# Input projection of a diffusion block: two chunks in one written order, weights loaded by GpSimd, first norm reordered

## The chip, the core and the metric

The kernel runs on one core of a Trainium2 chip. The metric is the device time of one execution in microseconds; a kernel's time is the median of several runs. The core has five engines that run beside each other, each with its own stream of instructions: TensorE (matmul; PE in the profile, PEld for its weight loads), VectorE (DVE), ScalarE (ACT), GpSimd (POOL) and SyncE (SP), which here only issues DMAs. They meet through semaphores. Matmuls write PSUM, eight banks of 128 x 512 numbers; everything else lies in SBUF, which has 128 partitions.

## The reference

One layer of a diffusion backbone over 512 latent tokens of width 2048 with 256 context tokens. What the change touches is its head:

```python
mod_l = (jax.nn.silu(c) @ w_ada[l] + b_ada[l])[:, None, :]
sh_a, sc_a, gt_a, sh_f, sc_f, gt_f = jnp.split(mod_l, 6, axis=-1)
h_l = modulate(rms_norm(x, g_mix_norm[l]), sh_a, sc_a)      # h * (1 + scale) + shift
qa_l, kva_l, kr_l, cb_l, cc_l, ch_l = split_projection(h_l @ w_in[l])
```

Here x is 512 x 2048 and w_in 2048 x 3904 (31 blocks of 128 columns, the last padded). After it come a low-rank attention with the context, a gated short convolution, an output projection, and a gated MLP (5504 wide) with a convolution, all in float32.

## The kernel before, in words

Activations lie transposed: 16 tiles `xs[j]` of 128 channels by 512 tokens. Each float32 factor is split into a high and a low part (`h`, `l`; fp32r), and a product takes three matmuls: high by high, high by low, low by high (`mm3`, L187 to L189). ScalarE makes the high part of a weight group (`split`, L166: up to four blocks of 128 x 128, 512 columns), VectorE the low part (L167).

**Modulation.** `mod` has 96 columns of 128 numbers. Column t is a dot product of a 128 x 2048 slab of w_ada (1 MB, loaded as two halves, the `ada` tiles, four of which fit in SBUF) with `sv`, Silu of c laid over all partitions. VectorE does it as two operations of 128 x 1024 with an accumulator (L241) and a tiny addition (`total`, L235). Tile j of h needs columns 16 + j (scale) and j (shift): `prep(j)` issues the four dots, scales x by the norm's factor `rl` on VectorE (L435), applies scale and shift on ScalarE (L438), and splits the result (L337, L338).

**Start.** SP loads io (identity and ones), c, sixteen x tiles, c_ctx, the small vectors `sm`, then ada halves and weights, in one queue. TensorE spreads c and c_ctx over the partitions by matmuls with a row of ones (L413), ScalarE takes Silu of them (L414). For the norm ScalarE squares each x tile and VectorE adds it to a sum (L354, L355); TensorE adds that over the partitions (`rs`, L316), ScalarE takes the root, VectorE the reciprocal, TensorE transposes it back (L299), and a copy of that is `rl`.

**Projection.** Its depth of 16 tiles is cut in three chunks, of 2, 4 and 10 (`KCH`), so that it can begin when two tiles of h are there. In each chunk the first six column blocks (`G`) are done row by row, tile after tile of h, into six PSUM banks; the other 25 one after another. Chunk one's results are copied to `acc` by ScalarE (L539), later ones added to it by VectorE (L541). Weights come by SP in loads of up to 1 MB into two buffers `raw`. The `prep`s of later tiles stand in a table after certain blocks (`todo`). A scheduler sets each engine's order; the instructions marked with `keep` hold the order in which they were written among themselves, and so do the loads that SP issues in the first two chunks. In chunk three VectorE also does the 64 dots of the context's modulation (`ctx_mods`, L530).

**Later places.** `late_dot` does the remaining 56 columns of `mod` beside attention and the output projection; `sv` is stored to HBM (`sv_d`) for the MLP stage, which reads it back; `ufr` are the first weights of the MLP.

Of the kernel before, what the change touches and what calls it, by code (L numbers as in the profile page):

```python
# [10 lines left out]
F32 = mybir.dt.float32  # L11
F32R = mybir.dt.float32r
AF = mybir.ActivationFunctionType
ALU = mybir.AluOpType
# [17 lines left out]
G = 6  # L32

# [39 lines left out]
def block_kernel(ctx, tc, xt, ctxt, ctxn, c, c_ctx, w_ada, small, w_in, w_inc, w_q, w_kv, w_out,  # L73
# [55 lines left out]
    def first_banks(nm):  # L129
        turn[:] = 5, None  # L130
        r = [sml(f"{nm}{g}") for g in range(4)]
        b = big(f"{nm}4")
        return r + [b[:, :512], b[:, 512:]]
# [15 lines left out]
    def load(src, n, name):  # L149
# [5 lines left out]
        fetch_to(raw[:, :n], src)  # L155
# [77 lines left out]
    def total(col, t, dst):  # L233

        V.scalar_tensor_tensor(out=dst, in0=col[:, 0:1], scalar=col[:, 1:2], in1=s("b_ada", t), op0=ALU.add, op1=ALU.add)  # L235

    def dot_v(raw, vec, t, dst, nm):

        col = tiny(2, f"dv{nm}{t}")
        for i, r in enumerate(raw):  # L240
            V.scalar_tensor_tensor(out=r, in0=r, scalar=1.0, in1=vec[:, i * 1024:(i + 1) * 1024], op0=ALU.mult, op1=ALU.mult, accum_out=col[:, i:i + 1])  # L241
# [158 lines left out]
    with ExitStack() as pa:  # L400
# [4 lines left out]
        def silu_rows(src, dst, nm):  # L405

            row = wp.tile([P, 2048], F32, tag="raw", bufs=2, name=nm)[0:1, :]
            fetch_to(row, src)
            for g in range(4):
                if g % 2 == 0:  # L410
                    both = big(f"{nm}{g}")
                ps = both[:, (g % 2) * 512:(g % 2 + 1) * 512]
                PE.matmul(ps, ones[0:1, :], row[:, g * 512:(g + 1) * 512], start=True, stop=True)  # L413
                A.activation(dst[:, g * 512:(g + 1) * 512], ps, AF.Silu)  # L414
# [7 lines left out]
        hl = {}  # L422

        def mods(j):
            ada(16 + j)
            ada(j)

        def prep(j):
            mods(j)
            modulate(j)  # L430

        def modulate(j):

            xr = xs[j]
            keep(V.tensor_tensor(out=xr, in0=xr, in1=rl, op=ALU.mult))  # L435
            sc = tiny(1, f"sc{j}")
            scale_of(sc, s("g_mix", j), mod[:, 16 + j:17 + j])
            A.activation(xr, xr, AF.Identity, bias=mod[:, j:j + 1], scale=sc)  # L438
            hl[j] = hilo(xr, T, f"h{j}")


        SP.dma_start(io, consts[:, KCW:])
        silu_rows(c, sv, "c")
        xs = []
        ssq = None
        for j in range(NK):
            xs.append(t2([P, T], F32, f"xr{j}"))
            fetch_to(xs[j], xt[:, j * T:(j + 1) * T])
            ssq = add_squares(ssq, xs[j], T, f"xs{j}")
        silu_rows(c_ctx, svc, "cc")  # L450
        fetch_to(sm, small)
        rms([ssq], D, T, rl)
# [1218 lines left out]
```

## Time and profile before

| what | value |
|---|---|
| runs, median (lowest to highest) | 2132.49 us (2132.07 to 2137.19) |
| the profiled execution, its time | 2139.37 us |
| its span | 2137.6 us |
| granted TensorE clock, mean | 0.993 |
| TensorE busy | 2091.0 us, 98% |
| VectorE busy | 1826.5 us, 85% |
| ScalarE, GpSimd busy | 1047.5 us, 117.2 us |
| first projection matmul | at 29.63 us |
| first matmul of chunk three | at 171.23 us |

In rows of the timeline the first number is the start in us, the second the duration, then engine, line, operation, output<-inputs and shapes; in brackets the idle time of the engine just before, and what ended it. In rows by stretches each engine has its busy time and in brackets its instructions, then come the granted clock as a share, the DMA engines' busy share and GB/s. Matmuls overlap: a row's duration is longer than the distance to the next start, and the distance is the cost.

### The profile page before, as it was taken

Reading aid. Unit: us, or ns where it says so; the run is one execution under the profiler, and the core shown is the slowest. Engines: PE = TensorE matmul, PEld = TensorE weight load, DVE = VectorE, ACT = ScalarE, POOL = GpSimd, SP = SyncE. Lnnn points to the kernel's source line nnn. Section 1 sums busy time; section 2 is a strip of 40 time slices with the busy share of each in tenths; the row PEclk is TensorE's granted clock in tenths of the full one; section 3 lists DMA queues with packets and bytes.
Section 4 is the critical chain, followed back from the end, with each engine's and each line's share of the span. In section 5 each row is a group of like instructions: output and inputs, shape, how many; then the busy total and the mean of one; then the engine's idle time right before and its main releaser. Section 6 shows DMA issues by size and latency. Waiting matters only on the chain.

```text
span 2137.6 us, 35318 instructions
## 1 busy us (share of the span) xinstructions
PE 2091.0 (98%) x13268; PEld 1881.8 (88%) x13268; DVE 1826.5 (85%) x3024; ACT 1047.5 (49%) x1715; POOL 117.2 (5%) x144
## 2 busy tenths in 40 slices
PE   7999999999999999999999999999999999999997
PEld 4688788888988888999999999999999889999997
DVE  7998987778896989898999999999999658888887
ACT  5533333555552337565555555555655433333445
POOL 0000000000000100011000000000000000000000
PEclk9999999999999999999999999999999999999999
DMA  8989886334459986577788888788888989878684
GB/s 331 343 279 329 276 275 195 126 128 152 166 188 353 348 283 220 142 217 207 230 238 232 233 233 244 224 234 234 235 229 229 362 306 307 250 231 239 197 236 134
DMA packets 170177, 513.75 MB, mean 240 GB/s; under 512 B 18963, under 2 KB 23315, under 8 KB 164371
## 3 DMA queue, kind: packets, MB, share of 16 engines
q1 hardware_dynamic: 133364, 418.14, 57.7%
q0 software_dynamic: 17408, 59.25, 14.1%
q10 hardware_dynamic: 19232, 34.09, 4.2%
q8 instruction: 104, 1.70, 0.3%
q14 instruction: 69, 0.56, 0.1%
HBM read 464.22 MB, written 46.14 MB: 239 GB/s over the span
## 4 chain that ended last, share of the span: by engine, by line
PE 90%; DVE 4%; DMA 3%; ACT 2%; issue 1%; SPq 0%; DVEq 0%; ACTq 0%; POOLq 0%
PE pp L187 4%; PE pp L189 4%; PE pp L188 4%; PE d L187 1%; PE o L187 1%; PE d L188 1%; PE o L188 1%; PE d L189 1%; PE o L189 1%; PE uf L187 1%; PE uf L189 1%; PE uf L188 1%; PE of L187 1%; PE of L188 1%; PE of L189 1%; PE pf L188 1%
## 5 line engine op out<-in xcount | busy, mean ns | idle before, releaser
L1151 POOL DMA_DIRECT2D u_s<-in_w_up x80 | 68.6, 857 | 684.0 <-DMA u_s<-in_w_up 378.1
L263 DVE SCALAR_TENSOR_TENSOR ada<-ada,sv 128x1024 f32<-128x1024 f32 x68 | 82.1, 1220 | 11.4 <-DMA ada<-in_w_ada 11.2
L166 ACT CAST w_0h<-rw 128x512 fp32r<-128x512 f32 (+1 forms) x63 | 38.3, 618 | 108.3 <-PE pp L188 67.6
L241 DVE SCALAR_TENSOR_TENSOR ada<-ada,sv 128x1024 f32<-128x1024 f32 x64 | 77.6, 1220 | 2.2 <-DMA ada<-in_w_ada 2.1
L530 DVE SCALAR_TENSOR_TENSOR ada<-ada,svc 128x1024 f32<-128x1024 f32 x64 | 76.0, 1219 | 2.5 <-DMA ada<-in_w_ada 2.4
L167 DVE TENSOR_TENSOR w_0l<-rw,w_0h 128x512 fp32r<-128x512 f32 (+1 forms) x63 | 42.7, 683 | 22.8 <-ACT w_0h L166 22.6
L263 DVE SCALAR_TENSOR_TENSOR ra<-ra,sv 128x1024 f32<-128x1024 f32 x44 | 52.5, 1219 | 1.1 <-DMA ra<-in_w_ada 1.1
L1265 DVE TENSOR_TENSOR u<-u,u_s 128x1024 f32<-128x1024 f32 x40 | 48.8, 1220 | 0.7 <-DMA u_s<-in_w_up 0.5
L1266 DVE TENSOR_TENSOR u<-u,u 128x1024 f32<-128x1024 f32 x40 | 48.7, 1218 | 0.0
L793 POOL TENSOR_TENSOR gr<-gr,half 128x8 f32<-128x8 f32 x4 | 10.1, 2524 | 630.1 <-DVE gr L792 538.2
L764 ACT CAST pth<-t 128x384 fp32r<-128x384 f32 x64 | 28.6, 485 | 26.4 <-PE t L761 26.4
L1075 DVE TENSOR_TENSOR tp<-a,tp 128x256 fp32r<-128x256 f32 x90 | 37.7, 419 | 3.3 <-ACT tp L1074 3.3
L1074 ACT CAST tp<-a 128x256 fp32r<-128x256 f32 x90 | 35.7, 403 | 5.5 <-DMA yl6h<-y_d 4.2
L1038 ACT ACTIVATE g<-g 128x512 f32<-128x512 f32 x43 | 27.3, 634 | 18.3 <-DVE g L1032 18.0
L541 DVE TENSOR_TENSOR acc<-acc,pp 128x512 f32<-128x512 f32 x50 | 34.1, 683 | 2.1 <-PE pp L189 2.1
L765 DVE TENSOR_TENSOR ptl<-t,pth 128x384 fp32r<-128x384 f32 x64 | 33.2, 550 | 2.6 <-ACT pth L764 2.6
L745 DVE TENSOR_REDUCE mn<-s 128x1 f32<-128x768 f32 x32 | 30.4, 953 | 4.9 <-PE s L734 4.6
L1030 ACT ACTIVATE g<-cg,sm 128x512 f32<-128x512 f32 x40 | 32.6, 815 | 0.0
L1030 ACT ACTIVATE a<-ca,sm 128x512 f32<-128x512 f32 x40 | 32.1, 802 | 0.0
L748 ACT ACTIVATE p<-s,mn 128x768 f32<-128x768 f32 x32 | 29.3, 916 | 1.6 <-DVE mn L745 1.3
L1031 DVE SCALAR_TENSOR_TENSOR g<-cg,sm,g 128x511 f32<-128x511 f32 x40 | 29.8, 746 | 0.0
L1032 DVE SCALAR_TENSOR_TENSOR g<-cg,sm,g 128x511 f32<-128x511 f32 x40 | 29.8, 746 | 0.0
(10238 smaller groups left out, 8925.0 us busy)
## 6 DMA issues: line engine op xcount, KB each, us to landing
ada<-in_w_ada SPq DMA_DIRECT2D x196, 512.0 KB, 5.7
u<-in_w_up SPq DMA_DIRECT2D x120, 512.0 KB, 8.9
w<-t_d SPq DMA_DIRECT2D x161, 256.0 KB, 5.3
u_s<-in_w_up SPq DMA_DIRECT2D x80, 512.0 KB, 4.0
u_s<-in_w_up POOLq DMA_DIRECT2D x80, 512.0 KB, 9.6
t_d<-tp ACTq DMA_DIRECT2D x126, 256.0 KB, 5.9
v<-in_w_dnw SPq DMA_DIRECT2D x72, 384.0 KB, 5.1
ra<-in_w_ada SPq DMA_DIRECT2D x22, 1024.0 KB, 4.8
```

The costliest lines, as they stand in the source:

```text
L166: A.copy(out=hi[:, :n], in_=raw[:, a:a + n])
L167: V.tensor_tensor(out=lo[:, :n], in0=raw[:, a:a + n], in1=hi[:, :n].bitcast(F32), op=ALU.subtract)
L187: PE.matmul(ps, w[0], x[0], start=first, stop=False, skip_group_check=on_top)
L188: PE.matmul(ps, w[0], x[1], start=False, stop=False, skip_group_check=on_top)
L189: PE.matmul(ps, w[1], x[0], start=False, stop=last, skip_group_check=on_top)
L241: V.scalar_tensor_tensor(out=r, in0=r, scalar=1.0, in1=vec[:, i * 1024:(i + 1) * 1024], op0=ALU.mult, op1=ALU.mult, accum_out=col[:, i:i + 1])
L263: keep(V.scalar_tensor_tensor(out=r, in0=r, scalar=1.0, in1=svs[i], op0=ALU.mult, op1=ALU.mult, accum_out=lc[:, t % 4:t % 4 + 1] if i else ...
L530: keep(V.scalar_tensor_tensor(out=raw[q], in0=raw[q], scalar=1.0, in1=svc[:, q * 1024:(q + 1) * 1024], op0=ALU.mult, op1=ALU.mult, accum_o ...
L1030: A.activation(u, src, AF.Identity, bias=s("fb", m), scale=s("fw", 86 + m))
L1151: G_.dma_start(r[-1], src[more], accum_op=ALU.add)
L1265: V.tensor_tensor(out=a11, in0=a11, in1=s1, op=ALU.add)
L1266: V.tensor_tensor(out=a12, in0=a12, in1=a11, op=ALU.add)
```

## The change

The first two chunks are written out as one stream of groups of up to four blocks, with every instruction of VectorE, ScalarE and TensorE kept in that order. Chunk one's row-by-row part has eight column blocks instead of six (`GCH`; the host's layout of w_in follows). A group's weights are split two groups ahead of its matmuls. `raw` loads go through GpSimd's DMA queue, in all three chunks, except the very first, which SP brings in two halves; the first GpSimd load stands behind a tiny copy on GpSimd that waits for `mod`'s column 17. Five steps of `preps` (four dots, a low part) are dealt out among the groups; tiles 14 and 15 come in chunk three.

At the start, io and c are loaded by ScalarE's queue; c_ctx is no longer spread by TensorE but loaded over all partitions by one DMA in chunk two. The Silu's table is loaded at once. The squares are summed in two parts; the transposed factor is used for x tile 0 straight from PSUM; ScalarE writes the high parts of tiles 0 and 1 directly. 27 matmuls on a copy of x (`warm`) into a bank that nobody reads (`idle`) stand among the norm's. The store of `sv` is kept in its written place, after the last `late_dot`.

TensorE's start, before; `c` and `cc` are the two rows being spread, `rs` the norm's sums (L316) and transposes (L299):

```order
L413 MATMUL c_108<-c,io 128x512
L413 MATMUL cc_194<-cc,io 128x512
L413 MATMUL cc_199<-cc,io 128x512
L413 MATMUL cc_194<-cc,io 128x512
L413 MATMUL cc_199<-cc,io 128x512
L316 MATMUL rs<-io,xs0t 128x1 x4
L299 MATMUL rs<-io,rr 128x128 x4
L187 MATMUL pf_222<-h0h,wf_0h 128x512
```

And now:

```order
L421 MATMUL c_106<-c,io 128x512
L510 MATMUL idle<-warm,ones_r 128x512 x14
L514 MATMUL rs<-io,xs_161 128x1 x4
L510 MATMUL idle<-warm,ones_r 128x512 x7
L514 MATMUL rs<-io,xs_229 128x1 x4
L510 MATMUL idle<-warm,ones_r 128x512
L541 MATMUL rs<-io,rr 128x128 x4
L510 MATMUL idle<-warm,ones_r 128x512 x5
L727 MATMUL pf_296<-h0h,w0h 128x512
```

The `cc` matmuls are gone from ahead of the norm's, and the idle ones have come in.

VectorE between the last square and tile 1's low part, now (`ada` rows are dots, L682 low parts of weights, L474 of h):

```order
L523 TENSOR_TENSOR xs_229<-xs_229,xs_233 128x512
L539 RECIPROCAL rr<-rr 128x4
L454 SCALAR_TENSOR_TENSOR ada_149,dv_216<-ada_149,sv 128x1024
L243 SCALAR_TENSOR_TENSOR mod<-dv_216,sm 128x1
L454 SCALAR_TENSOR_TENSOR ada_151,dv_259<-ada_151,sv 128x1024
L545 TENSOR_TENSOR xr_114<-xr_114,rs 128x512
L454 SCALAR_TENSOR_TENSOR ada_153,dv_259<-ada_153,sv 128x1024
L243 SCALAR_TENSOR_TENSOR mod<-dv_259,sm 128x1
L682 TENSOR_TENSOR w0l<-rf_155,w0h 128x512
L461 SCALAR_TENSOR_TENSOR sc_280<-mod,sm 128x1
L474 TENSOR_TENSOR h0l<-xr_114,h0h 128x512
L682 TENSOR_TENSOR w1l<-rf_155,w1h 128x512
```

Three of tile 0's four dots now stand behind the reciprocal; before, all four stood ahead of it.

The weight loads of the first chunks, which stood on SP among the ada loads, are GpSimd's first work after its constants:

```order
L705 COPY late<-mod 128x1
L159 DMA rw_368<-in_w_in 128x2048
L159 DMA rw_469<-in_w_in 128x2048
L159 DMA rw_585<-in_w_in 128x1792
L159 DMA rw_709<-in_w_in 128x1536
L159 DMA rw_779<-in_w_in 128x1536
```

Nothing but these loads and that copy is in GpSimd's stream until attention.

The diff, cut to its core:

```diff
+GCH = [8, 6, 6]
...
-        def silu_rows(src, dst, nm):
+        def broadcast_row(src, nm):
 
             row = wp.tile([P, 2048], F32, tag="raw", bufs=2, name=nm)[0:1, :]
-            fetch_to(row, src)
+            A.dma_start(row, src)
+            r = [sml(f"{nm}{g}") for g in range(4)]
...
+        def scaled(j, by):
+
+            x, sc = xs[j], tiny(1, f"sc{j}")
+            keep(V.scalar_tensor_tensor(out=sc, in0=mod[:, 16 + j:17 + j], scalar=1.0, in1=s("g_mix", j), op0=ALU.add, op1=ALU.mult))
+            if by is not None:
+                keep(V.tensor_tensor(out=x, in0=x, in1=by, op=ALU.mult))
+            hl[j] = tuple(t2([P, T], F32R, f"h{j}{z}") for z in "hl")
+            if j < 2:
+                keep(A.activation(hl[j][0], x, AF.Identity, bias=mod[:, j:j + 1], scale=sc))
+            keep(A.activation(x, x, AF.Identity, bias=mod[:, j:j + 1], scale=sc))
+            if j >= 2:
+                keep(A.copy(out=hl[j][0], in_=x))
...
+        def preps(js):
+            for j in js:
+                for t in (16 + j, j):
+                    for i in range(2):
+                        dot(t, i)
+                        if (t, i) == (j, 1):
+                            scaled(j, rl)
+                        yield
+                low(j)
+                yield
+
+        A.dma_start(io, consts[:, KCW:])
+        cps = broadcast_row(c, "c")
+        keep(A.activation(tiny(1, "silu"), eps, AF.Silu))
...
+        while len(xs) < 12:
+            x_load_in()
+        ada_half()
+        while len(xs) < NK:
+            x_load_in()
+        fetch_to(sm[:, :112], small[:, :112])
+        for _ in range(3):
+            ada_half()
+        raw0 = load(w_in[:, :2 * GCH[0] * P], 2 * GCH[0] * P, "rf00", halves=True)
...
+            if j == 13:
+                dot(16, 0)
+                warm_up(4)
+                sums(parts[0], True, False)
+                warm_up(3)
+            elif 8 <= j:
+                warm_up(2)
+        keep(A.activation(tiny(1, "root"), eps, AF.Sqrt))
+        sums(parts[1], False, True)
...
+        def split_group(i):
+            ci, bs, off, size, b = stream[i]
+            if off not in raws:
+                raws[off] = load(w_in[:, off:off + size * P], size * P, f"rw{off}", G_)
+            n = len(bs) * P
+            pool, bufs = (p_sb, 1) if i % 5 == 4 else (wp, 4)
+            hi, lo = (pool.tile([P, 512], F32R, tag="w" + z, bufs=bufs, name=f"w{i}{z}") for z in "hl")
+            src = raws[off][:, b * P:b * P + n]
+            keep(A.copy(out=hi[:, :n], in_=src))
+            keep(V.tensor_tensor(out=lo[:, :n], in0=src, in1=hi[:, :n].bitcast(F32), op=ALU.subtract))
+            ready[i] = hi, lo
...
+        for i, (ci, bs, off, size, b) in enumerate(stream):
+            if i < 2:
+                for _ in range(2):
+                    next(one)
+                if i == 1:
+                    keep(G_.tensor_copy(out=tiny(1, "late"), in_=mod[:, 17:18]))
+            else:
+                for n in range(len(ready), min({2: 4}.get(i, i + 3), len(stream))):
+                    split_group(n)
+                    if n == 2:
+                        next(one)
...
+            for key in out_of:
+                evac_now(*key, banks.pop(key))
+            if ci == 0 and i >= 2:
+                for _ in range(1 + (i % 3 != 0)):
+                    if not {2, 3, 4, 5} <= done:
+                        next(todo)
+            elif ci == 1 and 13 not in done:
+                next(todo)
+                if b + 4 >= size or size == 12:
+                    if 13 not in done:
+                        next(todo)
+            if ci == 1 and i == 24:
+                fetch_to(svc, c_ctx[0].partition_broadcast(P))
...
-    SP.dma_start(sv_d, sv)
+    keep(SP.dma_start(sv_d, sv))
```

260 lines of the change are left out of this document (171 added, 89 removed).

## The prediction

> **What bounds the kernel now.** I read the page's busy shares first, then the busy time by stretches of the first 180 us.
>
> ```profile
> span 2137.6 us, 35318 instructions
> PE 2091.0 (98%) x13268; PEld 1881.8 (88%) x13268; DVE 1826.5 (85%) x3024; ACT 1047.5 (49%) x1715; POOL 117.2 (5%) x144
> 30.00:40.00 10.00, 9.23 (x27) 6.17 (x26) 8.54 (x18) 2.89 (x5) 0.00 (x0) 1.00 0.82 326
> 40.00:50.00 10.00, 10.00 (x43) 8.15 (x44) 8.58 (x18) 4.95 (x9) 0.00 (x0) 1.00 0.81 257
> 50.00:60.00 10.00, 6.86 (x22) 4.67 (x21) 8.56 (x15) 5.34 (x10) 0.00 (x0) 0.76 1.01 403
> 60.00:70.00 10.00, 9.32 (x37) 7.20 (x35) 7.36 (x16) 4.93 (x9) 0.00 (x0) 0.90 0.73 258
> 100.00:120.00 20.00, 20.00 (x88) 16.21 (x87) 20.00 (x38) 6.56 (x12) 0.00 (x0) 1.00 0.83 281
> 180.00:200.00 20.00, 20.00 (x87) 16.21 (x87) 14.04 (x25) 10.82 (x19) 0.00 (x0) 1.00 0.89 309
> ```
>
> The columns are PE, PEld, DVE, ACT, POOL (busy us, instructions), clock, DMA share, GB/s. TensorE is the bound of the whole, with 46.6 us (2137.6 - 2091.0) not busy. From 100 us it is full, 88 matmuls in 20 us; in 30 to 70 us it does 129 in 40 us. That front part is what the change rewrites. The timeline there:
>
> ```profile
> 15.67 7.16 PE L413 MATMUL cc<-cc,io 1*128 1x512 f32 x8 [3.72 <-DMA cc<-in_c_ctx]
> 19.02 0.69 DVE L355 TENSOR_TENSOR xs0t<-xs0t,xs 128x512 f32<-128x512 f32 x1
> 22.76 1.86 PE L316 MATMUL rs<-io,xs0t 128*128 128x1 f32 x8
> 28.11 0.81 ACT L438 ACTIVATE xr<-xr,mod,sc 128x512 f32<-128x512 f32 x1 [1.04 <-DVE xr L435]
> 28.96 0.62 ACT L337 CAST h0h<-xr 128x512 fp32r<-128x512 f32 x1
> 29.63 2.07 PE L187 MATMUL pf<-h0h,wf_0h 128*128 128x512 f32 x4 [3.21 <-ACT h0h L337]
> 44.05 0.39 PE L189 MATMUL pp<-h0h,w_0l 128*128 128x512 f32 x1
> 51.26 0.40 PE L188 MATMUL pp<-h1l,w_0h 128*128 128x512 f32 x1
> 52.88 0.62 ACT L166 CAST w_0h<-rw 128x512 fp32r<-128x512 f32 x1 [5.96 <-DMA rw<-in_w_in]
> 57.30 0.80 PE L187 MATMUL pp<-h0h,w_0h 128*128 128x512 f32 x1 [1.23 <-ACT acc L539]
> 58.32 0.63 PE L189 MATMUL pp<-h0h,w_0l 128*128 128x512 f32 x1
> 61.31 0.63 PE L187 MATMUL pp<-h1h,w_0h 128*128 128x512 f32 x1
> 171.23 0.39 PE L187 MATMUL pf<-h6h,wf_0h 128*128 128x512 f32 x1
> ```
>
> The squares were summed at 19.71 us (19.02 + 0.69), but the matmuls that sum them over the partitions (`rs`) start at 22.76: they stand behind those that spread c_ctx (`cc`). The first projection matmul is at 29.63. Between 44.05 and 51.26 lie 31 starts, 0.2326 us each; between 58.32 and 61.31 lie 7, 0.427 each, where the granted clock fell to 0.76 after the waits at 52 to 57 us, which end with weights that came late (ScalarE waited 5.96 us).
>
> Chunks one and two have 31 x 6 x 3 = 558 matmuls, 129.8 us at 0.2326. The matmul at 171.23 has 546 projection matmuls ahead of it in program order, so that 558 are done at 171.23 + 12 x 0.2326 = 174.0. So 174.0 - 29.63 - 129.8 = **14.6 us** are lost between the first matmul and there, and what comes later waits little. At most these 14.6 and some of the 29.6 ahead of them can be won.
>
> **The start.** Removed ahead of the norm: the c_ctx row's eight passes (7.16 us of TensorE) and four Silus; SP's loads of io and c go to ScalarE's queue, so x starts one issue earlier (it began at 1.58, after io at 0.75); but half an ada tile goes ahead of the last four x tiles, 0.52 MB or 1.3 us at the 402 GB/s of
>
> ```profile
> 10.00:20.00 10.00, 6.28 (x8) 2.11 (x7) 8.83 (x15) 8.17 (x16) 0.00 (x0) 1.00 1.04 402
> 0.75 0.40 SPq L442 DMA_DIRECT2D io<-in_consts  x1
> 1.58 9.56 SPq L145 DMA_DIRECT2D xr<-in_xt  x16
> 6.23 1.28 ACT L414 ACT_TABLE_LOAD   x1
> 6.25 0.69 DVE L355 TENSOR_TENSOR xs0t<-xs0t,xs 128x512 f32<-128x512 f32 x1 [5.33 <-ACT xs L354]
> 8.68 10.25 DVE L355 TENSOR_TENSOR xs0t<-xs0t,xs 128x512 f32<-128x512 f32 x13 [1.73 <-ACT xs L354]
> 99.95 1.22 DVE L241 SCALAR_TENSOR_TENSOR ada<-ada,sv 128x1024 f32<-128x1024 f32 x1
> 101.09 0.08 DVE L241 DVE_READ_ACCUMULATOR ada<-ada,sv 128x1 f32 x1
> 101.09 0.69 DVE L167 TENSOR_TENSOR w_0l<-rw,w_0h 128x512 fp32r<-128x512 f32 x1
> 101.70 1.28 DVE L541 TENSOR_TENSOR acc<-acc,pf 128x512 f32<-128x512 f32 x2
> ```
>
> The adds take 0.79 us each (10.25 / 13), a dot 1.14 before the next starts, a 128x512 VectorE operation 0.60. The first add was at 6.25 and then waited 1.73 for ScalarE, which loaded the Silu's table at 6.23; now the table is loaded first. Thirteen adds from about 5.5 end near 15.9, the first dot near 17.1, the last add (last x near 17) near 18.2. Sums 0.9 to 1.9, square root and reciprocal 0.6, so 20 to 20.5. Then VectorE has, ahead of the first matmul, two dots, the scaling of x, one dot, `w0l`, two tiny totals: 3 x 1.15 + 2 x 0.60 + 0.4 = 5.1, and ScalarE's one pass that writes h0h itself 0.8. First matmul at **26.3**, 3.3 earlier. Bounds: 25.6 (x is in on time), 29.3 (the seven idle matmuls ahead of the second sum run at 0.427 instead of 0.2326, 1.4 us, and the sums at the slow end).
>
> **The second x tile.** 24 matmuls on h0 last 5.6, to 31.9. h1 needs, on VectorE after `w1l`, four dots, totals, the scaling: 4 x 1.15 + 0.4 + 0.6 = 5.6; then ScalarE writes h1h, x and w2h (0.8 + 0.8 + 0.6): 36.4. Idle: **4.5** (3.5 to 5.5). The order puts w2h last, so it cannot be hidden. I then take one slow stretch of 11 matmuls, 11 x 0.195 = **2.1** (0 to 4): waits of this kind brought one in the rows above. The 27 idle matmuls themselves cost nothing; TensorE waits there anyway.
>
> The Trainium skill (TensorE: Matmul & The Clock Gate, "What's actually happening") says that about 3.4 us of idleness halve the clock, and as much activity restores it. By it the idle matmuls, which end some 4 us before h0h, would not keep the first row fast, and the sum would keep the 2.1; the drop to 0.76 after shorter waits agrees in kind.
>
> **Weights by GpSimd.** In the old order a weight load stands on SP behind ada loads that wait for VectorE; now it is alone on its queue. The nearest rows:
>
> ```profile
> ada<-in_w_ada SPq DMA_DIRECT2D x196, 512.0 KB, 5.7
> rw<-in_w_in SPq DMA_DIRECT2D x9, 1024.0 KB, 7.9
> rw<-in_w_in SPq DMA_DIRECT2D x25, 640.0 KB, 6.2
> u_s<-in_w_up POOLq DMA_DIRECT2D x80, 512.0 KB, 9.6
> L1151 POOL DMA_DIRECT2D u_s<-in_w_up x80 | 68.6, 857 | 684.0 <-DMA u_s<-in_w_up 378.1
> ```
>
> GpSimd's own rows are loads that add into a tile which another load fills, so 9.6 is an upper bound; I take 8 (6 to 10). The first load is held by a tiny copy on `mod`'s column 17, at about 31, so it lands near 40, when w4 is wanted at 41 to 42. Later a buffer has four groups, 48 matmuls or 11.2 us, between its last split and its next use. **0** (0 to 4).
>
> The Trainium skill (SBUF — State Buffer, "SBUF: two separate sides") warns that GpSimd cannot write its descriptors while VectorE runs an operation in a two-port mode. The 857 ns in the row above, with VectorE busy, do not show that; if it bit here, it would be the slower rival below.
>
> **VectorE in the two chunks.** In chunk two, per four groups (48 matmuls, 11.2 us): 4 splits, 4 additions to acc, 4 dots, one scaling and one low part: 10 x 0.60 + 4 x 1.15 + 0.35 = 10.95 us. That just fits; in order with waits between I charge **1.5** (0 to 6). Tiles 14 and 15 move behind chunk two: 8 dots and 4 operations, 12 us, covered by chunk three, where VectorE is 5.96 us idle in 180 to 200 alone; if uncovered they cost up to 4.
>
> **The store of sv** moves from 16 us, where it shares the queue, to just ahead of the first up weights:
>
> ```profile
> 808.34 13.00 SPq L1136 DMA_DIRECT2D ufr<-in_w_up_first  x13
> 810.00:812.00 2.00, 1.50 (x13) 1.26 (x11) 1.20 (x5) 0.37 (x1) 0.00 (x0) 1.00 0.96 352
> 814.96 0.83 ACT L1023 CAST ufw0h<-ufr 128x768 fp32r<-128x768 f32 x1
> 815.83 0.39 PE L187 MATMUL uf<-hf0h,ufw0h 128*128 128x256 f32 x1 [0.88 <-ACT ufw0h L1023]
> ```
>
> TensorE waits there for ufw0h. 1.05 MB at 0.4 MB/us is 2.6 us of a full queue, of which the norm at 811 to 815 hides some: **1.0** (0 to 2.6).
>
> **Sum.** 26.3 + 129.8 + 4.5 + 2.1 + 0 + 1.5 = 164.2 against 174.0: 9.8 won, 1.0 given back, 8.8. The profiled execution took 2139.4 us (span 2137.6), so 2130.6 there; the median of the runs is 2132.5, so **2124**. Good ends: 25.6 + 129.8 + 3.5 = 158.9, 15 won, 2117. Bad ends: 29.3 + 129.8 + 5.5 + 4 + 6 = 174.6, nothing won, 2133.
>
> **Rivals.**
> *Half of it.* The norm's chain keeps its length (29.3), since the idle matmuls stand in TensorE's order ahead of the sums, and VectorE, now in one order, paces the chunks: 174.0 - (29.3 + 129.8 + 4.5 + 2.1 + 3) = 5.3, less 1.0: about 4, 2128. For it: the 10.95 of 11.2 us. Against: VectorE at 20.00 of 20 still kept TensorE full before.
> *Given back.* The front is faster, but a later stage, tied to transfers, starts earlier and waits longer: 2132. Against: TensorE shows 90% or more in nearly every slice after it.
> *Slower.* GpSimd's loads become the bound in chunk three: 25 loads of ten blocks, 30 matmuls or 7.0 us each, in two buffers. A buffer's round is the landing time plus about 2 us of splits, so from 12 us of landing on (2 x 7.0 - 2) TensorE waits; at 13.5 it is (15.5 / 2 - 7.0) = 0.75 a load, 19 us, less the 8.8: 2143. For it: the 9.6 us for half a megabyte. Against: 6.2 for the same loads on SP.
>
> **How the numbers follow.** The forecast 0.66, half of it 0.14, given back 0.10, slower 0.10. A run of this kernel tells 0.3%, 6.4 us, from no change. Nearly all of the forecast and a little of the second case are beyond that: faster 0.67; same 0.24; slower 0.09. The range runs from the good ends to no change, 2117 to 2132.5; what is left out is mostly the slower case.
>
> **What would show it.** The first projection matmul near 26.3; a gap of 4 to 5 us before h1's first matmul; the matmul of chunk three's first row near 164; GpSimd's loads landing in 6 to 10 us; ufw0h some 1 us later against hf0h than before. I am wrong if GpSimd's loads take over 12 us, if waits for VectorE's low parts fill chunk two, or if chunk two ends early and the end does not move.

## The result, and the profile after

The changed kernel takes 2164.59 us (median of five runs, 2161.53 to 2166.70) against 2132.49 for the kernel before in the same series: a ratio of 1.014, 95% interval 1.0128 to 1.0153. It is 32 us slower; 2124 was forecast. The profiled execution took 2166.65 us, its span is 2164.9, 27.3 more than before.

The head of its page, busy time by engine:

```profile
span 2164.9 us, 35371 instructions
PE 2100.3 (97%) x13295; PEld 1887.6 (87%) x13295; DVE 1826.7 (84%) x3024; ACT 1048.2 (48%) x1715; POOL 140.2 (6%) x187
```

VectorE and ScalarE have the work they had (1826.5 and 1047.5 before). TensorE has 27 more matmuls, and 64.6 us (2164.9 - 2100.3) in which it is not busy, against 46.6. So nothing grew; things wait. The timeline after, TensorE, VectorE and ScalarE, in the places that the prediction named:

```profile
27.70 1.95 PE L727 MATMUL pf<-h0h,w0h 128*128 128x512 f32 x4 [4.22 <-ACT h0h L466]
38.22 2.08 PE L727 MATMUL pf<-h1h,w2h 128*128 128x512 f32 x4 [3.12 <-ACT w2h L681]
...
113.21 0.68 DVE L463 TENSOR_TENSOR xr<-xr,rl 128x512 f32<-128x512 f32 x1
113.93 0.81 ACT L467 ACTIVATE xr<-xr,mod,sc 128x512 f32<-128x512 f32 x1 [10.94 <-DVE xr L463]
114.78 0.62 ACT L469 CAST h8h<-xr 128x512 fp32r<-128x512 f32 x1
115.30 0.61 ACT L681 CAST w26h<-rw 128x512 fp32r<-128x512 f32 x1
115.95 0.69 DVE L682 TENSOR_TENSOR w26l<-rw,w26h 128x512 fp32r<-128x512 f32 x1 [2.05 <-ACT w26h L681]
115.97 0.50 PE L727 MATMUL pp<-h2h,w26h 128*128 128x512 f32 x1 [2.09 <-ACT w26h L681]
129.33 0.69 DVE L682 TENSOR_TENSOR w30l<-rw,w30h 128x512 fp32r<-128x512 f32 x1 [2.06 <-ACT w30h L681]
186.29 0.79 PE L195 MATMUL pf<-h6h,wf_0h 128*128 128x512 f32 x1 [3.00 <-ACT wf_0h L174]
190.72 0.63 PE L727 MATMUL pp<-h4h,w46l 128*128 128x512 f32 x1
...
411.95 0.47 PE L195 MATMUL pp<-h6h,w_0h 128*128 128x512 f32 x1 [2.40 <-ACT gq L373]
432.40 2.08 PE L389 MATMUL qr<-xq,kc 128*128 128x512 f32 x2 [6.77 <-ACT xq L826]
```

Read the six rows from 113.21 on as one ring. VectorE scales tile 8. ScalarE, which had been idle for 10.94 us, applies scale and shift, casts h8h, and only then casts w26h, because that is the written order. VectorE, whose next instruction is w26's low part, waits 2.05 us for that cast; TensorE waits 2.09 for the same. ScalarE waits for VectorE and VectorE for ScalarE once per tile: a round from w26l to w30l takes 13.38 us (129.33 - 115.95), in which TensorE has 48 matmuls, 11.2 us. The same round by stretches; the third busy time is VectorE's, 11.26 us:

```profile
115.95:129.33 13.38, 13.21 (x48) 10.00 (x48) 11.26 (x22) 3.51 (x7) 0.53 (x1) 0.87 0.64 212
```

The waits have a second price. The same kernel by stretches; behind PE, PEld, DVE, ACT and POOL stands the granted clock:

```profile
27.70:190.70 163.00, 144.00 (x558) 109.21 (x559) 132.13 (x251) 64.65 (x111) 9.18 (x16) 0.94 0.76 265
116.00:121.00 5.00, 5.00 (x14) 3.73 (x15) 5.00 (x9) 1.48 (x3) 0.00 (x0) 0.66 0.38 157
400.00:420.00 20.00, 17.61 (x83) 14.18 (x82) 19.33 (x38) 9.74 (x18) 0.00 (x0) 1.00 0.47 157
420.00:440.00 20.00, 13.23 (x51) 9.92 (x51) 11.48 (x25) 8.99 (x19) 0.00 (x0) 0.83 0.19 65
```

Behind the wait at 116 TensorE is busy throughout and starts 14 matmuls in 5 us, at a clock of 0.66; full speed would be 21.

**Where the 27.3 us arose.** In the matmul at 190.72 TensorE begins its 559th projection matmul (at 186.29 four of chunk three's went ahead of ten of chunk two's), so that the first two chunks' 558 are done at 190.7, against 174.0: 16.7 us. From there to `qr`, the first rotary matmul of attention, it takes 241.7 us (432.4 - 190.7), against 234.2 (408.2 - 174.0): 7.5 more. Behind `qr` it is 1732.5 against 1729.4: 3.1. In the first two chunks 190.7 - 27.7 - 129.8 = 33.2 us are lost, against 14.6. TensorE's waits are 18.6 of them: 3.1 for w2h, 3.0 for wf_0h, 12.5 at the weights of chunk two. The low clock is at most 9.8: the mean granted clock of these 163.0 us is 0.94 (0.06 x 163.0). What is left, some 5 us or more, are matmuls that start further apart at a full clock, most of them right behind a wait (0.34 and 0.39 us instead of 0.23 behind the one that ends at 169.26); why wasn't traced.

### The profile page after: what moved, and what is told of

Same layout as the page of the kernel before. It is cut to its first block, busy times and chain, and to the rows that moved or that the text cites. A ratio compares the mean times of both kernels' runs of the same rounds, so it can differ in the third digit from the quotient of the medians.

```text
span 2164.9 us, 35371 instructions
## 1 busy us (share of the span) xinstructions
PE 2100.3 (97%) x13295; PEld 1887.6 (87%) x13295; DVE 1826.7 (84%) x3024; ACT 1048.2 (48%) x1715; POOL 140.2 (6%) x187
## 4 chain that ended last, share of the span: by engine, by line
PE 76%; issue 13%; DMA 5%; DVE 4%; ACT 1%; POOL 1%; DVEq 0%; POOLq 0%; SPq 0%; ACTq 0%
PE pp L195 2%; PE pp L197 2%; PE pp L196 2%; PE d L195 1%; PE d L196 1%; PE d L197 1%; PE uf L195 1%; PE uf L196 1%; PE uf L197 1%; DMA rw<-in_w_in 1%; PE t L935 1%; PE of L196 1%; PE of L195 1%; PE of L197 1%; DMA ada<-in_w_ada 1%
## 5 line engine op out<-in xcount | busy, mean ns | idle before, releaser
L626 DVE SCALAR_TENSOR_TENSOR ada<-ada,svc 128x1024 f32<-128x1024 f32 x64 | 75.6, 1219 | 3.0 <-DMA ada<-in_w_ada 3.0
L454 DVE SCALAR_TENSOR_TENSOR ada<-ada,sv 128x1024 f32<-128x1024 f32 x64 | 76.7, 1219 | 0.0
L467 ACT ACTIVATE xr<-xr,mod,sc 128x512 f32<-128x512 f32 x16 | 13.0, 814 | 81.1 <-DVE xr L463 81.0
L1439 DVE TENSOR_TENSOR u<-u,u_s 128x1024 f32<-128x1024 f32 x40 | 48.8, 1219 | 0.9 <-DMA u_s<-in_w_up 0.9
L174 ACT CAST w_0h<-rw 128x512 fp32r<-128x512 f32 x25 | 15.5, 620 | 50.9 <-DMA rw<-in_w_in 30.3
L159 POOL DMA_DIRECT2D rw<-in_w_in x37 | 19.7, 533 | 304.7 <-DVE w_8l L175 109.5
L1212 ACT ACTIVATE g<-g 128x512 f32<-128x512 f32 x43 | 27.3, 634 | 17.8 <-DVE g L1206 17.7
L939 DVE TENSOR_TENSOR ptl<-t,pth 128x384 fp32r<-128x384 f32 x64 | 33.2, 548 | 2.7 <-ACT pth L938 2.7
L922 ACT ACTIVATE p<-s,mn 128x768 f32<-128x768 f32 x32 | 29.3, 916 | 1.6 <-DVE mn L919 1.3
L1205 DVE SCALAR_TENSOR_TENSOR a<-ca,sm,a 128x511 f32<-128x511 f32 x40 | 29.8, 745 | 0.0
```

The source lines that it names most:

```text
L454: keep(V.scalar_tensor_tensor(out=r, in0=r, scalar=1.0, in1=svs[i], op0=ALU.mult, op1=ALU.mult, accum_out=dv[t][:, i:i + 1]))
L626: keep(V.scalar_tensor_tensor(out=raw[q], in0=raw[q], scalar=1.0, in1=svc[:, q * 1024:(q + 1) * 1024], op0=ALU.mult, op1=ALU.mult, accum_o ...
L1205: V.scalar_tensor_tensor(out=u[:, 1:], in0=src[:, :T - 1], scalar=s("fw", m), in1=u[:, 1:], op0=ALU.mult, op1=ALU.add)
L1439: V.tensor_tensor(out=a11, in0=a11, in1=s1, op=ALU.add)
```

## The experiments

A table first, of one profiled execution each: TensorE's first projection matmul, the time from which the 558 are done, the first `qr`, the way between these two, the span, and the median of the runs. The kernel before ran beside each group, with medians of 2132.5 to 2136.0.

| run | what it is | first | 558 done | qr | between | span | median |
|---|---|---|---|---|---|---|---|
| | before | 29.6 | 174.0 | 408.2 | 234.2 | 2137.6 | 2132.5 |
| | the change | 27.7 | 190.7 | 432.4 | 241.7 | 2164.9 | 2164.6 |
| a_cast | casts a group ahead | 27.3 | 174.7 | 421.0 | 246.3 | 2150.6 | 2151.8 |
| a2_cast_low | and h's low part later | 27.4 | 172.9 | 420.2 | 247.3 | 2151.7 | 2147.7 |
| d_sp | loads on SP | 27.0 | 187.8 | 438.5 | 250.7 | 2172.0 | 2166.7 |
| b_ctx | context's dots from row one | 27.5 | 191.7 | 443.7 | 252.0 | 2172.7 | 2172.5 |
| c_both | a_cast and b_ctx | 27.5 | 176.4 | 425.5 | 249.1 | 2155.1 | 2155.5 |
| e_mid | dots dealt faster | 27.0 | 191.0 | 437.7 | 246.8 | 2167.1 | 2167.2 |
| f_a2_mid | a2 and e_mid | 27.2 | 172.0 | 419.9 | 247.9 | 2150.7 | 2151.4 |
| m_short | a2, tiles 14, 15 cut | 27.7 | 172.7 | 416.3 | 243.6 | 2146.1 | 2151.3 |
| n_back14 | a2, tiles 14, 15 back | 27.1 | 178.3 | 422.3 | 244.0 | 2155.5 | 2155.3 |
| k_back | and the dots back | 27.2 | 176.4 | 413.1 | 236.7 | 2146.5 | 2149.4 |
| s_depth | k_back, three groups ahead | 27.2 | 173.7 | 411.3 | 237.6 | 2140.9 | 2140.4 |
| p_pool3 | a2, GpSimd helps | 27.3 | 178.8 | 418.3 | 239.5 | 2150.3 | 2152.7 |
| l_pool | k_back, GpSimd helps | 27.4 | 185.4 | 422.6 | 237.2 | 2149.2 | 2150.9 |
| v_best | s_depth, two waits less | 29.7 | 178.1 | 420.0 | 241.9 | 2145.7 | 2147.0 |
| w_best | and no idle matmuls | 26.9 | 173.9 | 412.3 | 238.4 | 2136.4 | 2141.8 |
| j_noidle | the change, no idle matmuls | 27.6 | 191.1 | 430.1 | 239.0 | 2159.9 | 2161.7 |
| q_cc | before, without c_ctx at the start | 27.5 | 173.1 | 410.7 | 237.6 | 2141.1 | 2141.0 |
| u_ccsv | and sv stored late | 27.9 | 171.7 | 407.1 | 235.4 | 2138.8 | 2139.1 |

Runs of one kernel lie up to 14 us apart here, so that 3 us between two rows say little; the milestones of a trace say more than its end. j_noidle is a single run. Some expectations count from chunk three's first matmul, 186.3 in the changed kernel, and so have 246 where the table has 241.7. No version of the change is faster than the kernel before: the nearest, s_depth and w_best, have ratios of 1.0026 and 1.0027, with intervals above 1.

**The ring, and the loads.** Theory 1 is the ring. Theory 2 holds that VectorE's work paces the chunks anyway, theory 3 the prediction's slower rival, that GpSimd's loads are late. a_cast moves a cast, and nothing else:

```diff
-        def split_group(i):
...
+        def high(i):
...
             keep(A.copy(out=hi[:, :n], in_=src))
+            highs[i] = hi, lo, src, n
+
+        def split_group(i):
+            high(i)
+            hi, lo, src, n = highs[i]
             keep(V.tensor_tensor(out=lo[:, :n], in0=src, in1=hi[:, :n].bitcast(F32), op=ALU.subtract))
             ready[i] = hi, lo
+            if i >= 5:
+                high(i + 1)
```

> The changed kernel, but from the sixth weight group on ScalarE makes the high part of a group one group earlier, so that it stands ahead of the scaling of an x tile instead of behind it. Theory 1 (the loss in chunk two is a ring: VectorE scales x, ScalarE applies scale and shift, casts h, and only then casts the weights that VectorE wants next; 2.05 us of VectorE seven times): the seven waits of 2.05 us before the weights' low parts go, 14.4 us, but h's low part, which follows, now waits for its own cast, 1.43 less the 0.6 of the operation put ahead, 0.8 seven times: about -8.5 us, 2156 (2151 to 2160). Theory 2 (VectorE's own work paces the chunks, the waits are slack): 2165. Theory 3 (GpSimd's loads are late): 2165.

In a2_cast_low, `low(j)` stands behind the first dot of the next tile:

> As the run before, and h's low part stands one dot later in VectorE's order, behind the first dot of the next tile. Theory 1: of the 22 us that VectorE waits in front of low parts (7 x 2.05 and 5 x 1.53) nearly all go; a round of four groups falls from 13.3 us to VectorE's busy 11.25, against TensorE's 11.2, so that both bound it: -15 us, 2149 (2144 to 2153). Theory 2 and theory 3: 2165.

d_sp takes `G_` out of the three calls of `load`:

> The changed kernel with every weight load of the three chunks back on SP's queue. Theory 3 (GpSimd's loads are the cause, as the rival of the prediction had it): much of the loss goes, 2140 to 2150. Theories 1 and 2 (they land in time): no gain, 2165, or some us more where a weight load now stands behind ada loads that wait for VectorE (2163 to 2172).

Measured: 2151.8, 2147.7 and 2166.7. Theory 1 stands, and the gain is larger than it said: 12.8 and 16.9 us of the medians, since some of the low clock goes with the waits (in a_cast TensorE's waits in the two chunks fall from 18.6 to 9.4 us, and the mean clock there rises from 0.94 to 0.97). Theory 2, which had both versions at 2165, falls. Theory 3 falls too: with the loads on SP the median is the same (chunk two ends 2.9 us earlier, the way to `qr` is 9.0 longer), and in the changed kernel GpSimd's landed no later than SP's, which took 6.3 and 8.4 us in d_sp:

```profile
rw<-in_w_in POOLq DMA_DIRECT2D x25, 640.0 KB, 5.7
rw<-in_w_in POOLq DMA_DIRECT2D x8, 1024.0 KB, 7.6
```

In a_cast's timeline the same round of tile 8:

```profile
110.65 0.68 DVE L463 TENSOR_TENSOR xr<-xr,rl 128x512 f32<-128x512 f32 x1
111.25 0.68 DVE L691 TENSOR_TENSOR w26l<-rw,w26h 128x512 fp32r<-128x512 f32 x1
111.36 0.81 ACT L467 ACTIVATE xr<-xr,mod,sc 128x512 f32<-128x512 f32 x1 [9.60 <-DVE xr L463]
112.87 0.69 DVE L474 TENSOR_TENSOR h8l<-xr,h8h 128x512 fp32r<-128x512 f32 x1 [0.34 <-ACT h8h L469]
174.73 0.50 PE L195 MATMUL pf<-h6h,wf_0h 128*128 128x512 f32 x1 [2.16 <-ACT wf_0h L174]
```

w26l now follows the scaling at once; 0.34 us are left, at h8l. In a2_cast_low two scalings that follow each other, of tiles 9 and 10:

```profile
116.32 0.68 DVE L463 TENSOR_TENSOR xr<-xr,rl 128x512 f32<-128x512 f32 x1
127.48 0.68 DVE L463 TENSOR_TENSOR xr<-xr,rl 128x512 f32<-128x512 f32 x1
```

A round of 11.16 us, which is TensorE's own pace; VectorE is busy 11.09 of it:

```profile
116.32:127.48 11.16, 11.16 (x50) 9.05 (x49) 11.09 (x24) 3.52 (x6) 0.53 (x1) 1.00 0.82 284
```

The prediction's 10.95 us of VectorE's work against TensorE's 11.2 was right as a sum, and false as a time, since the order put 2 us of waiting into it.

**Behind chunk two.** Both versions end chunk two as early as the kernel before, and their spans are still 13 and 14 us longer: the way to `qr` is 12 to 13 us longer. TensorE waits at 411.95 and 432.40, in the rows above. What is late there is the context. Its last dot before and after (the row of the accumulator that closes it):

```profile
354.55 0.08 DVE L530 DVE_READ_ACCUMULATOR ada<-ada,svc 128x1 f32 x1
```

```profile
402.86 0.08 DVE L626 DVE_READ_ACCUMULATOR ada<-ada,svc 128x1 f32 x1
```

The diff has `if q >= 5:` ahead of `next(cm)`: the dots begin with chunk three's sixth row instead of the first. The prediction didn't price that line. b_ctx takes it back alone (`if q >= 0:`), c_both with the casts ahead, e_mid and f_a2_mid leave it and deal the dots out faster later on (`2 if i % 2 == 0` for `2 if i % 4 == 0`). Theory 4: the late dots are the whole of it.

> The changed kernel, but the context's dots begin with the first row of chunk three instead of the sixth, as before the change. Theory 1 (some 8 us of the loss arise behind chunk three, where the context's preparation is late on VectorE, ScalarE and SP: TensorE idle 2.40 and 6.77 us near 410 and 430, then slow to 437): about -8 us, 2156.5 (2153 to 2161), with chunk two's end still near 192. Rival (the dots are not what is late there; the gap comes from chunk two's late end, or moves to another wait): within 2 us of 2165.

> The cast one group earlier (measured alone 2151.8) and the context's dots from chunk three's first row (measured alone 2172.5, 8 slower). Theory 4 with a VectorE that has no room in the first rows of chunk three: the two add up, 2159 (2156 to 2163). Rival (those rows were short of room only because chunk two ended late and in lockstep): the seam's gap goes and nothing is given back, 2143 (2140 to 2147).

> The changed kernel with the context's dots dealt out faster in chunk three: two steps behind every second column block instead of every fourth; they still begin with the sixth row. Theory 4 (TensorE's gaps of 2.40 and 6.77 us and the slow stretch behind them, at the seam to attention, come from the context's dots, whose last one ends at 402.9 us, against 354.6 before the change): the last dot near 380, the gaps gone, -8 us, 2157 (2153 to 2160). Rival (VectorE has no room left in chunk three, so that dots done earlier only make the weights' low parts late, as they did where the dots began with the first row, 2172): 2163 to 2172.

> The cast one group earlier, h's low part one dot later (measured together 2147.7), and the context's dots dealt out two steps behind every second block. Theory 4: the seam's gaps of 2.4 and 4.3 us and the slow stretch behind them go, -7 us, 2141 (2137 to 2145). Rival (no room on VectorE): 2146 to 2155.

Measured: 2172.5, 2155.5, 2167.2, 2151.4. All four miss what theory 4 foresaw (c_both by half a microsecond): none is faster than the version it is built on, and b_ctx is 8 us slower. The rivals of b_ctx and c_both are missed too; those of e_mid and f_a2_mid, that VectorE has no room in chunk three, are hit. The gap at `qr` shrinks to 1.0 us in b_ctx and c_both and to 3.8 in e_mid, and the time comes back elsewhere. In b_ctx by stretches, and then what TensorE waited for longest in 190 to 320 us (us in total, times, longest):

```profile
240.00:260.00 20.00, 9.99 (x32) 7.27 (x33) 18.30 (x34) 4.26 (x9) 0.53 (x1) 0.74 0.79 269
```

```profile
PE pp L195 <- ACT w_0h L174: 8.3, 4, 5.2
PE pp L197 <- DVE w_0l L175: 3.2, 1, 3.2
```

With the dots and tiles 14 and 15 both in chunk three's first rows, the weights' parts come late there, and TensorE does 32 matmuls in 20 us.

**Tiles 14 and 15.** Theory 5: VectorE has no room in chunk three, work there costs its own length. m_short leaves out most of these tiles' eight dots, k_back prepares them in chunk two again and starts the dots with the first row, n_back14 only prepares them in chunk two:

```diff
-            elif ci == 1 and 13 not in done:
+            elif ci == 1 and 15 not in done:
                 next(todo)
-                if b + 4 >= size or size == 12:
-                    if 13 not in done:
+                if b + 4 >= size or size == 12 or b == 4:
+                    if 15 not in done:
                         next(todo)
...
-            if q >= 5:
+            if q >= 0:
```

> The cast one group earlier and h's low part one dot later (measured 2147.7 and, in another kernel, 2151.4), but the eight dots of tiles 14 and 15, which the change moved into chunk three, take 64 of 1024 columns, so that their modulation is wrong: some 8.5 us of VectorE's work is left out there (8 x 1.06). Theory 5 (VectorE has no room in chunk three and up to the seam; work put there costs about its own length, wherever it stands): -7 to -9 us, 2141 (2138 to 2144). Rival (the gaps at chunk three's start and at the seam come from the order of ScalarE, GpSimd or the loads there): within 3 us of 2149.

> The cast one group earlier, h's low part one dot later, tiles 14 and 15 prepared in chunk two again, and the context's dots from chunk three's first row, both as before the change. Theory 5: chunk two is paced by VectorE, which has 6 us idle in 100 to 175, and gets 12 us more: its end moves from 173 to 179 or later; chunk three then runs as before the change, without gaps: 2143 (2139 to 2147). Rival (something else of the change makes the gaps in chunk three): 2152 or more.

> The cast one group earlier, h's low part one dot later, tiles 14 and 15 prepared in chunk two again; the context's dots still begin with chunk three's sixth row. Theory 6a (the 12 us of the two tiles' dots are what chunk three has no room for): chunk three's first matmul to the first rotary matmul in 237 to 239 us, the end as with the dots put back too, 2149 (2146 to 2152). Theory 6b (the dots, five steps late, are what fails at the seam): 244 to 247 us, the end 2157 (2154 to 2160).

Measured: 2151.3, 2149.4, 2155.3. m_short's 8.5 us less work gave 3.7 on the way to `qr` and nothing in the median, as its rival had it, so theory 5 as a rule of conservation falls. k_back lies between theory 5's 2143 and the rival's 2152. n_back14 hit what 6b said: 244.0 on the way, 2155.3; with the dots back as well (k_back) it is 236.7, 2.5 from the kernel before. n_back14 and k_back by stretches:

```profile
175.00:200.00 25.00, 23.13 (x94) 18.32 (x93) 15.63 (x29) 10.39 (x18) 1.59 (x3) 0.93 0.79 275
200.00:230.00 30.00, 30.00 (x135) 24.41 (x133) 23.22 (x43) 12.48 (x22) 2.12 (x4) 1.00 0.74 255
380.00:400.00 20.00, 17.87 (x84) 14.34 (x82) 19.70 (x38) 8.99 (x17) 0.53 (x1) 1.00 0.39 125
```

```profile
175.00:200.00 25.00, 23.52 (x100) 18.80 (x101) 20.31 (x37) 13.83 (x23) 2.11 (x4) 1.00 0.91 339
200.00:230.00 30.00, 27.47 (x120) 21.96 (x119) 26.61 (x50) 8.62 (x16) 1.58 (x3) 1.00 0.91 316
380.00:400.00 20.00, 20.00 (x98) 16.56 (x97) 16.63 (x33) 11.11 (x22) 0.53 (x1) 1.00 0.27 74
```

The third busy time is VectorE's. With the dots from the sixth row on it is idle 16.2 us between 175 and 230 and full at 380 to 400, where attention's first inputs are made; with the dots from the first row it is idle 8.1 early and has 3.4 spare late. So each of the two moves spoils the other's place: the dots need the first rows, and the tiles, put there, crowd them out. Either alone doesn't mend the way to `qr`; both do. TensorE's wait at `qr` is 6.8 us in n_back14, where only the dots are late, and 1.0 in k_back. And with the dots from the first row in both, the tiles in chunk three cost 12.4 us on that way (c_both 249.1, k_back 236.7; where h's low part stands differs too, which made 1.0 between a_cast and a2_cast_low).

**More room for VectorE.** p_pool3 and l_pool give work of VectorE to GpSimd:

```diff
+        for j in range(1, NK):
+            keep(G_.tensor_tensor(out=xs[j], in0=xs[j], in1=rl, op=ALU.mult))
...
-            keep(V.tensor_tensor(out=hl[j][1], in0=xs[j], ...
+            keep((V if j < 2 else G_).tensor_tensor(out=hl[j][1], in0=xs[j], ...
```

> The cast one group earlier and h's low part one dot later; GpSimd, whose weight loads go back to SP's queue (measured alone: no difference), multiplies x tiles 1 to 15 by the norm's factor as soon as it is there, and makes the low parts of tiles 2 to 15. That takes 15 + 14 operations of 0.60 us, 17.4 us, off VectorE, two thirds of it in the first two chunks. Theory 5: chunk two ends at TensorE's own pace, near 165, and chunk three keeps its crowding: -9 us from 2149, 2140 (2135 to 2145). Rival (GpSimd's operations are slow or hinder VectorE): 2150 or more.

> As the run before, with tiles 14 and 15 in chunk two and the context's dots from chunk three's first row, as before the change. Theory 5: VectorE's 12 us fit into the room that GpSimd made in chunk two; chunk two ends near 170, chunk three runs as before the change: some 4 us under the kernel before, 2129 (2124 to 2136), the best of all. Rival: not under 2133.

Measured 2152.7 (ratio 1.0087) and 2150.9 (1.0073): the rival holds. p_pool3's groups in 27 to 60 us, GpSimd's first and then VectorE's (busy us, mean ns of one, idle before; the means of the dots hold two that start after GpSimd's last multiply):

```profile
L713 POOL TENSOR_TENSOR xr<-xr,rl 128x512 f32<-128x512 f32 x15 | 27.4, 1862 | 28.1 <-ACT rl L710 28.1
L454 DVE SCALAR_TENSOR_TENSOR ada<-ada,sv 128x1024 f32<-128x1024 f32 x9 | 17.2, 1937 | 0.0
L696 DVE TENSOR_TENSOR w5l<-rw,w5h 128x512 fp32r<-128x512 f32 x1 | 1.8, 1764 | 0.0
```

Around GpSimd's multiplies a dot takes 1937 ns on average instead of 1219 (2.27 to 2.32 us in six of the seven that run beside them, 1.21 in the other), and this low part 1764 instead of 690; h1's first matmul comes at 42.9 instead of 38.2.

s_depth splits weights three groups ahead (`i + 4` for `i + 3`, but 6 at the fourth group) in k_back's version; the store of `sv` is no longer kept:

> The cast one group earlier, h's low part one dot later, tiles 14 and 15 in chunk two, the context's dots from the first row (all this measured 2149.4); in addition the weights are split three groups ahead instead of two, and the store of sv is left to the scheduler, as before the change. Theory (VectorE's lookahead is too short where six additions stand together, TensorE waits 2.0 us for w25l, 1.5 for w46l; the store costs up to 3 us): -3 to -6 us, 2144.5 (2142 to 2147). Rival (VectorE is the bound of chunk two, lookahead moves nothing; the store is hidden): 2148 to 2151.

Measured 2140.4 us, ratio 1.0026 (1.0016 to 1.0036), the best version of the change: 9 us under k_back, more than expected. What TensorE waited for longest in chunks one and two of k_back, and of s_depth, apart from the waits for h0h, for w2h (2.2 and 3.4 us) and for chunk three's first weights (1.8 and 2.8):

```profile
PE pp L743 <- DVE w25l L696: 2.0, 1, 2.0
PE pp L743 <- ACT acc L704: 1.6, 1, 1.6
PE pp L743 <- DVE w46l L696: 1.5, 1, 1.5
```

```profile
PE pp L743 <- DVE w39l L696: 1.2, 1, 1.2
PE pp L743 <- DVE w43l L696: 0.9, 1, 0.9
```

Two things were changed and not taken apart. The earlier end of chunk two (2.7 us) is likely the lookahead's, since the store, left to the scheduler, is issued at 15.4 us there, in the start's queue. The store is counted below.

v_best takes two more waits away (w2h and w3h cast ahead of tile 1's scaling; the load of one lone group first in chunk two), w_best also the idle matmuls; j_noidle is the changed kernel without these:

> The version measured at 2140.4 (casts ahead, low part later, three groups of lookahead, tiles 14 and 15 and the context's dots where they were before the change), and two waits taken away: ScalarE casts w2h and w3h ahead of the second x tile's scaling instead of behind it, and chunk two's single-group load comes first instead of last, so that the buffer for chunk three's first weights is free a load earlier. Theory: of TensorE's 3.4 us ahead of h1's first matmul 1 to 2 go, of the 2.8 us ahead of chunk three nearly all: -4, 2136.5 (2133 to 2139), not told from the kernel before. Rival (VectorE paces the chunks and takes the gain back): 2139 to 2142.

> As the run before, without the 27 idle matmuls. Theory (TensorE's clock at the first row is low with and without them): within 2 us of the run before. Rival (they cost or win, as one look at the changed kernel without them, 2161.7 against 2164.6, may say): 3 us or more faster.

> The changed kernel without the 27 idle matmuls. Theory (seven of them stand between the norm's two sums, the last square is added at 18.73 us and the second sum starts at 20.15, behind them): the first projection matmul 1.3 us earlier, 26.4, its first row slow in any case (0.43 us a matmul); the end within 3 us of 2165. Rival (they keep the clock up): first row slower for longer, chunk one later by 2 us or more.

Measured: 2147.0 (1.0053), 2141.8 (1.0027), and 2161.7 in a single run. v_best missed by 10 us, and w_best came out as its rival had it, 5 us faster than v_best; the two waits shrank (to 0.6 and 1.6 us), and in their place stand 4.7 us at `w_0l` in chunk three, 3.1 at an `acc` and 3.0 at w26l. The idle matmuls aren't free, as the reciprocal of the norm's root shows, in v_best and in w_best (in brackets VectorE's wait before it, which begins soon after the last square is added):

```profile
23.45 0.18 DVE L544 RECIPROCAL rr<-rr 128x4 f32<-128x4 f32 x1 [3.79 <-ACT rr L542]
```

```profile
20.66 0.18 DVE L544 RECIPROCAL rr<-rr 128x4 f32<-128x4 f32 x1 [2.25 <-ACT rr L542]
```

1.5 us between the two waits (a later x makes up the rest of the 2.8); it is 0.4 in the changed kernel, whose wait is 2.70 against 2.26 in j_noidle. So the seven that stand ahead of the second sum delay it. In j_noidle the first matmul came hardly earlier for that, 27.6 where 26.4 was expected, since the last square was later too.

**Parts of the change alone, on the kernel before.** q_cc drops the spreading of c_ctx from the start and loads svc in chunk two; u_ccsv also keeps the store of `sv` in its place:

> The kernel before, with one part of the change alone: c_ctx isn't spread by TensorE at the start, but loaded over all partitions in chunk two, and one Silu taken of it there. Theory (the norm's sums stood 3 us behind the spreading of c_ctx, and VectorE paces the front from there): the first projection matmul at 27 instead of 29.6, the end 2.5 us earlier, 2132 against 2134.5 (ratio 0.9988). Rival (the front is paced by loads, and the start's gain is eaten by chunk two): ratio 1.000.

> As the run before, and the store of sv kept in its written place, behind the last late dot, as in the change. Theory (the store of 1 MB leaves the start's queue, 2.6 us of it, and costs 1.0 at the first up weights): the first projection matmul no earlier than in the run before, the end 1 us later or the same: ratio 0.9985 to 0.9995. Rival: it delays the up weights by its whole 2.6 us: ratio 1.000 or more.

Measured: ratios 1.0031 (1.0021 to 1.0042) and 1.0020 (1.0007 to 1.0034). Both miss their theories; u_ccsv lies where its rival had it. In q_cc the first matmul does come at 27.5, 2.1 us earlier, chunk two's end 1.0, and the end is later. The waits of TensorE in 100 to 300 us of q_cc, all of them:

```profile
PE pp L189 <- DVE w_0l L167: 3.6, 1, 3.6
```

Before the change the one wait there is 1.1. It lies where chunk three goes from rows to blocks. Why the scheduler's order is worse there wasn't tried.

## Why the prediction was wrong, point by point

- **First matmul, 26.3 (25.6 to 29.3):** 27.7. The last square was added at 18.7 (18.2 foreseen) and VectorE waited 2.7 for the norm's root behind it (sums, root and reciprocal were to take 1.5 to 2.5). Mechanism right.
- **h1's gap, 4.5 (3.5 to 5.5):** 3.1, after a slower first row (granted clock 0.51 from 27.91 to 31.32; the idle matmuls did not keep it up). The 2.1 for one slow stretch was mis-sized: up to 9.8 us at a low clock up to chunk two's end. The prediction reasoned that waits bring such stretches, and then foresaw hardly any waits.
- **GpSimd's loads, 0:** right for the queue. They landed in 5.7 (640 KB) and 7.6 us (1024 KB), and on SP the time is the same. What the term missed is the buffer: the load of chunk three's first weights is issued only at 178.1, when w45l frees a `raw` buffer, and lands at 185.5, so that TensorE waits 3.0 us at 186.29 (2.4 in d_sp, on SP). The slower rival had the right sign for a wrong reason, which is luck.
- **VectorE in the two chunks, "just fits", 1.5 (0 to 6): the step that failed.** The sum of 10.95 us was right: VectorE is busy 11.26 us in the changed kernel's round and 11.09 in a2_cast_low's. It was a sum over one engine; ScalarE's order was not laid beside it. The rows of the change say scale, shift, cast h, then cast the weights, and the next low part is VectorE's next instruction. That is 0.81 + 0.62 + 0.61 us in series, readable before the run. Where 1.5 was charged, TensorE waited 12.5 us for chunk two's weights, and the low clock came on top; a_cast, which only moves the cast, ends chunk two 16.0 us earlier. "Half of it" named the pacer, but priced 3 us.
- **What the chunks lose in all, 8.1 instead of 14.6:** not reached without the ring either. a2_cast_low loses 172.9 - 27.4 - 129.8 = 15.7 us and s_depth 16.7, so that of the earlier start, 2.2 and 2.4 us, only 1.1 and 0.3 are left at chunk two's end. Where the rest of these waits comes from stays open.
- **Tiles 14 and 15, "covered by chunk three, up to 4": failed too.** What was left out is `q >= 5`: the dots moved to make way, and the work they make late is attention's first input. The way to `qr` is 7.5 us longer in the changed kernel and 12 to 13 once chunk two is mended, so that a part of the mended time is given back. k_back shows that the two moves together are the cause of nearly all of it (2.5 us are left); the split between them isn't additive.
- **The store of sv, 1.0 (0 to 2.6):** from `qr` to the end the 15 profiled kernels with the store kept late take 1730.8 us on average (1726.6 to 1733.5), the five others, the kernel before among them, 1727.8 (1724.1 to 1730.4). That is 3.0 us, just above the upper bound, but the kernels differ in more than the store and the two spreads overlap; u_ccsv, where it alone is added to q_cc, takes 1.3 more on that way and is no slower by its median. The size stays open.
- **The range** took VectorE's bound only up to 6 us, because nothing in the old trace showed VectorE waiting: there the scheduler had ordered both engines, and VectorE was busy 20.00 of 20 us. A written order takes that away, and its cost can't be read from a trace made without it.

## What to carry to other kernels

When an order is fixed by hand, walk the queues of all engines side by side and look for rings: an engine that waits for a result of the engine that waits for it, once per round; the sum of work per engine says nothing on that. Put the instruction that the other engine needs soonest ahead of the one that has to wait. And price every line of a diff that moves a start, `if q >= 5` too: work that is put off lands on whoever needs its result first.

## What the runs showed of the hardware

**VectorE and GpSimd hinder each other on SBUF operands.** In p_pool3, around GpSimd's multiplies of two SBUF tiles, VectorE's dots took 1937 ns on average instead of 1219 and a low part 1764 instead of 690. GpSimd's multiplies themselves took 1.26 to 2.31 us, 1862 ns on average. The Trainium skill (SBUF — State Buffer, "SBUF: two separate sides") says that a VectorE instruction with two SBUF inputs contends with a GpSimd instruction that reads SBUF, for an interface that one holds for the whole instruction; the dots and low parts have two such inputs, and the trace agrees. GpSimd's loads, issued beside the same operations in the changed kernel, showed none of it: the 40 dots from 60 to 190 us took 1219 ns on average.

**Waits of 1.6 us cost the clock, or don't.** In the changed kernel the clock fell behind a wait of 2.09 us that ends at 115.97 and behind one of 1.60 that ends at 142.66, and stayed at 1.00 behind one of 1.60 that ends at 169.26. The Trainium skill (TensorE: Matmul & The Clock Gate, "What's actually happening") names about 3.4 us of idleness for the halving; none of these waits was that long, so that here shorter ones were enough. What tells them apart is how much of a wait falls into one beat: in the clock records of these traces the granted clock changes only on a beat of 3.41 us. Here are, in pairs, the beat that holds most of each of the three waits and the beat behind it; the first busy time is TensorE's, and the clock stands third from the end:

```profile
113.19:116.61 3.42, 1.33 (x5) 0.50 (x4) 1.37 (x5) 2.64 (x5) 0.00 (x0) 1.00 0.97 335
116.61:120.02 3.41, 3.41 (x9) 2.66 (x9) 3.41 (x7) 0.87 (x2) 0.00 (x0) 0.50 0.40 165
140.50:143.91 3.41, 1.81 (x7) 0.90 (x6) 1.36 (x4) 3.26 (x6) 0.00 (x0) 1.00 0.91 334
143.91:147.33 3.42, 3.42 (x9) 2.64 (x8) 3.42 (x7) 0.26 (x1) 0.00 (x0) 0.50 0.30 122
167.81:171.22 3.41, 1.95 (x7) 1.35 (x8) 1.98 (x4) 2.93 (x6) 0.00 (x0) 1.00 0.75 259
171.22:174.63 3.41, 3.41 (x16) 2.76 (x15) 3.40 (x6) 0.00 (x0) 0.00 (x0) 1.00 0.25 85
```

TensorE is busy 1.33, 1.81 and 1.95 us of the three beats. Over all 20 traces, from 25 to 2100 us, beats at a full clock with TensorE busy for less than 45% were followed by a beat at half clock 96 times in 97, those from 45 to 55% 15 times in 32, and those above 55% twice in some 11800. These shares are counts over these kernels; why the clock follows them isn't shown.
